# Opening the first SwiGLU with P1 and P2 of four groups, a second level one pair earlier, and P7 moved ahead of P2 in the values

## Chip, cores and metric

The kernel runs on one core of one Trainium2 chip. Its time is device microseconds (us) of one launch; of several runs the median is given. The engines are named as in the profile: PE (TensorE, matmuls), PEld (its weight loads), DVE (VectorE), ACT (ScalarE), POOL (GpSimd) and SP (SyncE, which here issues the loads and stores).

## What is computed

One layer of a streaming encoder on 1024 tokens of width 1024, in float32:

```python
h = x + 0.5 * swiglu(rmsnorm(x, g1), w1_in, w1_out)      # first SwiGLU, d_ff = 2816
u = rmsnorm(h, g_mix)
q, k, v, g_ret, p, gates = split(u @ w_in)               # "values" below is v
...                                                      # retention, pooling, merge
h = h + merged @ w_out
h = h + 0.5 * swiglu(rmsnorm(h, g2), w2_in, w2_out)
out = rmsnorm(h, g_final)
# swiglu(x) = (silu(x @ w_in[:, :2816]) * (x @ w_in[:, 2816:])) @ w_out
```

## The kernel before

**One matmul in float32.** A product of 128 weight columns by 512 tokens over 128 channels is made from three matmuls (`mm3`, lines 176 to 180): weights and operand are each split into a rounded high part (a cast on ScalarE, line 158) and a remainder (a subtraction on VectorE, line 159; lines 162 and 163 do the same with a scale), and high x high, high x low and low x high are added in PSUM.

**Groups.** The input half of a SwiGLU (`ffn_in`, line 693) has 22 groups of 256 output rows: 128 gate rows and 128 up rows, by 1024 tokens, over 1024 channels. With channels, rows and tokens each halved, a group is a 2 x 2 block product, made by Strassen's scheme in Winograd's form (`strassen`, line 425) with seven products, P1 to P7, instead of eight. Weight operands are L11, L12, L22 and the combinations S1 to S4; token operands are R11, R21, R22 and the combinations T1 to T4, made once and kept in 28 buffers (`mv`). One product is 12 matmuls of 512 columns. P1 and P2 (L11 x R11, L12 x R21) need only tokens as they come; P6 needs T2, P7 T3, P5 T1, P4 T4, P3 R22. P1 stands in a bank `a`, is copied to a bank `b` where P6, P5 and P3 are added, and P2 is added to it in `a`.

**Second level.** Two neighbouring groups together have one product (P3 over R22, or P2 over R21) that is again a 2 x 2 block product, and `common` (line 531) makes it with seven half products of 256 columns, 42 matmuls, instead of two products of 24 matmuls of 512. It needs the blocks of R22 or of R21 and their differences (`blocks`), made once for all pairs and kept in buffers of the rings `tl` (4) and `t4` (9).

**Order in the first SwiGLU.** The first group is a plain one (`plain_group`, line 776): eight products of 12 matmuls, with no combinations, whose operands are R11, R21, R12, R22. Then `pairs_of_both` (line 610) takes the other 21: two groups side by side in the order P1, P2, P6, P7, P5, P4, P3 (`BY_OPERAND`), a third one alone, and nine pairs, of which the first three have a second level on P3 alone and the last six on both.

**Order of the work.** `Flow.run` takes the steps one by one: a step has a part that prepares its weights (done four steps ahead) and a body with its matmuls. Side work on the operands, norms and outputs waits in one queue, `flow`; after each body one piece of it is taken (two in some stages), and a body that needs an operand takes pieces until that operand is made. The order of instructions on each engine is fixed when the kernel is built, by this order as a priority, with later work moved up where an engine would wait; on the chip each engine keeps its order.

**Beginning.** Lines 1046 to 1069 load the plain group's weights and the halves of x (16 loads of 256 KB) from SP's queue and put the operands' work into `flow`, then eight `x_square` pieces (line 1069 on), which square x by tokens, and the norm's statistics: roots and a row of 1024 factors (`n1rb`), spread over the partitions with four matmuls. Before the row is there, a gate is copied out as it is and scaled at the group's end; then follow silu, the product with the up rows, and for each two groups the combinations that the output half needs (lines 746 to 758), stored to memory.

**Values.** The projection v (line 1222 on) is one block product of its own, its seven products in four steps each. P1, P6, P7 and P4 go into four banks `a`; P5, P3 and P2 into four banks `b`. The order was P1, P6 with P5, P3, P2, P7, P4. When P2 is done, the norm's statistics and the blocks of its R22 go into `flow`.

Of the kernel before, what the change touches and what calls it, by code (L numbers as in the profile page):

```python
# [90 lines left out]
def block_kernel(ctx: ExitStack, tc, x, x_tok, vecs, f1_in, f1_out, w_in, w_v, pool_w, w_ret, w_pool, w_o,  # L91
# [330 lines left out]
    class Group(list):  # L422
        pass

    def strassen(nx, wa, wb, name, evac, end, begin=None, shared=(), dest=None):

        t = {}

        def blocks():
            ra, rb = raw(f"{name}ra"), raw(f"{name}rb")
            load(ra, wa)
            load(rb, wb)
            t.update(L11=half(ra, 0), L12=half(ra, 1), L21=half(rb, 0), L22=half(rb, 1))
# [24 lines left out]

        def prod(dst, w, m, start, stop):
            for i in range(4):
                mm3(t[dst], parts(t["w", w], i), parts(nx.operand(m, i)), start and i == 0, stop and i == 3)

        def u(n):
            t[n] = c2(f"{name}{n}")
            return t[n]

        def b1():
            if begin:  # L470
                begin()
            t["a"] = bank(f"{name}a")
            prod("a", "L11", "R11", True, False)
            t["b"] = sum_bank(f"{name}b")
            with soon():
                copy(t["b"], t["a"])

        def b6():
            prod("b", "S2", "T2", False, False)
            with soon():  # L480
                copy(u("v"), t["b"])

        def fourth():

            if "b5" in t and "p7" in t:
                with soon():
                    evac((1, 1), t["b"], t["p7"])

        def b5():
            prod("b", "S1", "T1", False, False)  # L490
            t["b5"] = True
            fourth()

        def b7():
            t["e"] = bank(f"{name}e")
            prod("e", "S3", "T3", True, False)
            with soon():
                copy(u("p7"), t["e"])
            fourth()

        def b2():
            prod("a", "L12", "R21", False, True)
            with soon():
                evac((0, 0), t["a"], None)

        def b3():
            prod("b", "S4", "R22", False, True)
            with soon():
                evac((0, 1), t["b"], None)

        def b4():
            prod("e", "L22", "T4", False, True)
            with soon():
                evac((1, 0), t["e"], t["v"])

        def last(f):
            def go():
                f()
                t["ends"] = t.get("ends", 0) + 1
# [87 lines left out]

        return step[0], body

    def pairs_of_both(nx, groups, first, some):  # L610

        groups = list(groups)
        A, B = (g(()) for g in groups[:2])
        steps = [g[m] for m in first for g in (A, B)]
        n = 2
        if len(groups) % 2:
            C = groups[n](())
            steps += [C[m] for m in BY_SUM]
            n += 1
        tl_, t4_ = ("tl", N_TL), ("t4", N_T4)  # L620

        steps[-1] = then(steps[-1], nx.blocks("R22", [t4_, tl_, t4_], True))
        yield from steps
        for k, n in enumerate(range(n, len(groups), 2)):
            A, B = (g((2, 3) if k >= some else (3,)) for g in groups[n : n + 2])
            yield A[0]
            yield B[0]
            if k < some:
                yield A[4]
                yield then(B[4], nx.blocks("R21", [tl_] * 3, True)) if k == some - 1 else B[4]  # L630
            elif k > some:
                yield from common(nx, A, B, 2)

            yield from (A[3], A[1], B[3], B[1], A[2], B[2])
            if k != some:
                yield from common(nx, A, B, 3)
                yield A[6]
                yield B[6]
            else:
                yield from common(nx, A, B, 2)  # L640
                yield A[6]
                yield B[6]
                yield from common(nx, A, B, 3)
# [46 lines left out]
            yield prep, body  # L690


    def ffn_in(nx, w, ops, name, start=None):

        R, T, B, T4 = ops
        hid = {}
# [1 line left out]
        def group(g):  # L698
            gate_up = {}

            def dest(which):
                tile, j = which
                if tile not in gate_up:
                    gate_up[tile] = (tl if start and g == 0 else t4)(f"{name}{'gu'[tile]}{g}")
                return half(gate_up[tile], j)

            later = []
# [53 lines left out]

                flow.add(w1, w1b, w2, w3)

            if start and g == 0:
                return plain_group(nx, start, f"{name}{g}_", evac, end)
            return lambda shared: strassen(nx, w[g, 0], w[g, 1], f"{name}{g}_", evac, end, shared=shared, dest=dest)

        done = ops_done.setdefault(name, set())
        order = [g for k in range(FH) for g in (k, k + FH)]
        if start:  # L770
# [5 lines left out]
    def plain_group(nx, blocks, name, evac, end):  # L776

        t, w = {}, {}

        def step(o, i, j):  # L780


            def prep():
                if j == 0:
                    w[o, i] = weights(blocks[2 * o + i], f"{name}w{o}{i}")

            def body():
                if i == 0:
                    t[o] = bank(f"{name}{o}{j}")
                for k in range(4):  # L790
                    mm3(t[o], parts(w[o, i], k), parts(nx.operand(("R11", "R12", "R21", "R22")[2 * i + j], k)),
                        i == 0 and k == 0, i == 1 and k == 3)
                if i == 1:
                    evac((o, j), t[o], None)
                    if (o, j) == (1, 1):
                        end()

            return prep, body

        return [step(o, i, j) for j in range(2) for i in range(2) for o in range(2)]  # L800

    ops_done = {}

# [252 lines left out]
    load(lead[0], f1_in[0, 0, :, :H])  # L1056
# [164 lines left out]
    def values():  # L1221
# [690 lines left out]
```

## Time and profile before

| | us |
|---|---|
| median of 3 runs | 2156.06 |
| lowest and highest of them | 2154.53, 2156.15 |
| profiled execution | 2153.9 |
| span of its profile (first to last instruction) | 2152.1 |
| TensorE busy in the span | 2138.3 |
| VectorE busy | 1848.9 |
| ScalarE busy | 1092.7 |

The profile is of one execution. A row of the timeline gives start, duration, engine, line, operation, output <- inputs, and how many were merged (x), with the idle time before and what ended it in brackets. A row of the waits gives who waited for whom, the total, the number and the longest. A row of the windows gives a stretch, its length, and each engine's busy time in it with the number of instructions, then the granted TensorE clock, the DMA engines' busy share and GB/s. Names are those of the program without numbers: `a_` is the first SwiGLU's input half (`a_wS` a weight of a combination, `a_b`, `a_a`, `a_e`, `a_x`, `a_y` banks), `n1` its norm and operands (`n1R`, `n1T`), `vL` and `vS` the values' weights and banks.

### The profile page before, as it was taken

What the parts mean: (1) busy time and instruction counts of PE and PEld (TensorE: products, weight loads), DVE (VectorE), ACT (ScalarE), POOL (GpSimd) and SP (SyncE); (2) the same over time, 40 slices, a digit from 0 to 9 for tenths busy, and PEclk for the clock granted to TensorE, in tenths of its full rate; (3) what the DMA queues carried; (4) which work ended last, traced back from release to release, by engine and by line L of the source; (5) the groups of instructions that cost most, each with busy time, mean ns of one, the idle gap of its engine ahead of it and who ended that gap; (6) DMA issues with size and microseconds to landing.
All of it is one profiled execution on the core that took longest, in us unless ns stands there. A gap on an engine that the chain in (4) does not pass through costs nothing.

```text
span 2152.1 us, 29764 instructions
## 1 busy us (share of the span) xinstructions
PE 2138.3 (99%) x10686; PEld 1812.0 (84%) x10686; DVE 1848.9 (86%) x3248; ACT 1092.7 (51%) x2059; POOL 0.2 (0%) x4
## 2 busy tenths in 40 slices
PE   9999999999999999999999999999999999999998
PEld 7888888888887888888888898887888888888887
DVE  8798888997988689888888877899988888899796
ACT  8544444454654444444446754446644544445454
POOL 0000000000000000000000000000000000000000
PEclk9999999999999999999999999999999999999999
DMA  7232423585537233332336567634123232358542
GB/s 259 73 133 74 138 83 128 181 283 186 182 119 242 89 127 138 108 128 91 115 119 238 168 220 256 218 99 157 69 89 132 74 130 91 128 180 291 200 132 98
DMA packets 120131, 320.91 MB, mean 149 GB/s; under 512 B 13232, under 2 KB 17456, under 8 KB 119984
## 3 DMA queue, kind: packets, MB, share of 16 engines
q1 hardware_dynamic: 119408, 317.98, 43.0%
q8 instruction: 83, 1.36, 0.3%
q10 hardware_dynamic: 576, 1.05, 0.1%
q14 instruction: 64, 0.52, 0.1%
HBM read 228.27 MB, written 90.70 MB: 148 GB/s over the span
## 4 chain that ended last, share of the span: by engine, by line
PE 93%; DVE 3%; DMA 1%; ACT 1%; issue 1%; SPq 0%; DVEq 0%; ACTq 0%
PE c_b L178 2%; PE c_b L180 2%; PE c_b L179 2%; PE a_b L178 2%; PE a_b L179 2%; PE a_b L180 2%; PE c_e L178 2%; PE c_e L179 2%; PE c_e L180 2%; PE a_e L179 2%; PE a_e L178 2%; PE a_e L180 2%; PE c_a L179 1%; PE c_a L180 1%; PE c_a L178 1%; PE a_a L178 1%
## 5 line engine op out<-in xcount | busy, mean ns | idle before, releaser
L179 PE MATMUL c_b<-n3T,c_wS 128*128 128x512 f32 x176 | 68.5, 389 | 0.0
L180 PE MATMUL c_b<-n3T,c_wS 128*128 128x512 f32 x176 | 68.5, 389 | 0.0
L178 PE MATMUL c_b<-n3T,c_wS 128*128 128x512 f32 x176 | 68.1, 389 | 0.0
L178 PE MATMUL a_b<-n1T,a_wS 128*128 128x512 f32 x168 | 65.4, 389 | 0.0
L179 PE MATMUL a_b<-n1T,a_wS 128*128 128x512 f32 x168 | 65.4, 389 | 0.0
L180 PE MATMUL a_b<-n1T,a_wS 128*128 128x512 f32 x168 | 65.3, 389 | 0.0
L178 PE MATMUL a_a<-n1R,a_wL 128*128 128x512 f32 x120 | 46.7, 389 | 0.0
L179 PE MATMUL a_a<-n1R,a_wL 128*128 128x512 f32 x120 | 46.7, 389 | 0.0
L180 PE MATMUL a_a<-n1R,a_wL 128*128 128x512 f32 x120 | 46.7, 389 | 0.0
L179 PE MATMUL c_a<-n3R,c_wL 128*128 128x512 f32 x112 | 43.7, 390 | 0.0
L180 PE MATMUL c_a<-n3R,c_wL 128*128 128x512 f32 x112 | 43.6, 389 | 0.0
L178 PE MATMUL c_a<-n3R,c_wL 128*128 128x512 f32 x112 | 43.6, 389 | 0.0
L178 PEld LDWEIGHTS c_b<-n3T,c_wS 128*128 128x128 f32 x176 | 33.1, 188 | 6.9
L179 PEld LDWEIGHTS c_b<-n3T,c_wS 128*128 128x128 f32 x176 | 33.0, 188 | 6.9
L180 PEld LDWEIGHTS c_b<-n3T,c_wS 128*128 128x128 f32 x176 | 33.0, 188 | 6.8
L159 DVE TENSOR_TENSOR a_wS<-a_S,a_wS 128x512 fp32r<-128x512 f32 x45 | 30.8, 684 | 8.0 <-ACT a_wS L158 8.0
L180 PEld LDWEIGHTS a_b<-n1T,a_wS 128*128 128x128 f32 x168 | 31.5, 188 | 6.6
L178 PEld LDWEIGHTS a_b<-n1T,a_wS 128*128 128x128 f32 x168 | 31.5, 188 | 6.6
L179 PEld LDWEIGHTS a_b<-n1T,a_wS 128*128 128x128 f32 x168 | 31.5, 188 | 6.5
L159 DVE TENSOR_TENSOR c_wS<-c_S,c_wS 128x512 fp32r<-128x512 f32 x46 | 31.4, 682 | 3.7 <-ACT c_wS L158 3.6
L179 PE MATMUL c_e<-n3T,c_wL 128*128 128x512 f32 x88 | 34.4, 391 | 0.0
L178 PE MATMUL c_e<-n3T,c_wL 128*128 128x512 f32 x88 | 34.4, 391 | 0.0
(3109 smaller groups left out, 8059.6 us busy)
## 6 DMA issues: line engine op xcount, KB each, us to landing
c_ra<-in_f_in SPq DMA_DIRECT2D x22, 512.0 KB, 3.6
c_rb<-in_f_in SPq DMA_DIRECT2D x22, 512.0 KB, 4.3
a_ra<-in_f_in SPq DMA_DIRECT2D x21, 512.0 KB, 3.7
a_rb<-in_f_in SPq DMA_DIRECT2D x21, 512.0 KB, 4.5
t<-au SPq DMA_DIRECT2D x11, 512.0 KB, 4.1
b<-ag SPq DMA_DIRECT2D x11, 512.0 KB, 3.3
r<-au SPq DMA_DIRECT2D x11, 512.0 KB, 3.5
br<-r SPq DMA_DIRECT2D x11, 512.0 KB, 5.6
```

The lines of the kernel that those rows point to most:

```text
L159: tt(lo, src, hi.bitcast(F32), SUB)
L178: mm(dst, w[0], m[0], start=start, stop=False, skip_group_check=True)
L179: mm(dst, w[0], m[1], start=False, stop=False, skip_group_check=True)
L180: mm(dst, w[1], m[0], start=False, stop=stop, skip_group_check=True)
```

## The change

The first SwiGLU no longer has a plain group. Four groups (0, 11, 1, 12) make P1 and P2 first (`leading`): P1 goes from its bank to the half of the gate tile that P3 fills later, and is copied into bank `b` when P6 begins. Then the first two groups make their other products side by side, and the second two the rest of theirs as a pair with a second level on P3. The other nine pairs have second levels on both P2 and P3. The four gates stand in the ring `tl`, and `x_square` loads into `t4` instead. R12 isn't made any more. The loads at the beginning are ordered anew, and the work on R22 comes ahead of T2 in `flow`, with R22's own split last. The second SwiGLU is as it was. In the values, P7 comes before P2.

```diff
@@ strassen @@
-    def strassen(nx, wa, wb, name, evac, end, begin=None, shared=(), dest=None):
+    def strassen(nx, wa, wb, name, evac, end, begin=None, shared=(), dest=None, lead=None):
...
-                if n == "L11":
+                if "L11" not in t:
                     blocks()
-                elif n in ("S2", "S3") and "S1" not in t:
+                if n in ("S2", "S3") and "S1" not in t:
                     combine("S1", "L21", "L22", ADD)
...
+        def first(n):
+            def prep():
+                t["w", n] = weights(half(lead, n == "L12"), f"{name}w{n}")
+
+            def body():
+                if n == "L11":
+                    t["a"] = bank(f"{name}a")
+                    prod("a", n, "R11", True, False)
+                    with soon():
+                        copy(dest((0, 1)), t["a"])
+                else:
+                    b2()
+
+            return prep, body
+
         def b6():
+            if lead is not None:
+                t["b"] = sum_bank(f"{name}b")
+                with soon():
+                    copy(t["b"], dest((0, 1)))
             prod("b", "S2", "T2", False, False)
...
+        if lead is not None:
+            g[0], g[4] = first("L11"), first("L12")
@@ pairs_of_both @@
+    def leading(nx, groups):
+
+        A, B, C, D = (g(s) for g, s in zip(groups, ((), (), (3,), (3,))))
+        for m in (0, 4):
+            yield from (g[m] for g in (A, B, C, D))
+        rest = [g[m] for m in BY_OPERAND if m not in (0, 4) for g in (A, B)]
+        rest[-1] = then(rest[-1], nx.blocks("R22", [T4_, TL_, T4_], True))
+        yield from rest
+        yield from (C[3], C[1], D[3], D[1], C[2], D[2])
+        yield from common(nx, C, D, 3)
+        yield C[6]
+        yield then(D[6], nx.blocks("R21", [TL_] * 3, True))
...
-    def pairs_of_both(nx, groups, first, some):
+    def pairs_of_both(nx, groups, lead):
+
+        groups, some, n = list(groups), 0 if lead else 2, 4 if lead else 2
+        if lead:
+            yield from leading(nx, groups[:n])
+        else:
+            A, B = (g(()) for g in groups[:n])
...
@@ ffn_in @@
-                    gate_up[tile] = (tl if start and g == 0 else t4)(f"{name}{'gu'[tile]}{g}")
+                    gate_up[tile] = (tl if g in start and not tile else t4)(f"{name}{'gu'[tile]}{g}")
...
-            return chain(group(0), pairs_of_both(nx, (group(g) for g in order[1:]), BY_OPERAND, 3))
-        return pairs_of_both(nx, (group(g) for g in order), BY_OPERAND, 2)
+        return pairs_of_both(nx, (group(g) for g in order), start)
@@ beginning @@
-    ra, rb = raw("ra"), raw("rb")
-    lead = half(ra, 0), half(ra, 1), half(rb, 0), half(rb, 1)
+    lead = {g: raw(f"lead{g}") for g in (0, FH, 1, FH + 1)}
...
+    def leads(j, gs):
+        for g in gs:
+            load(half(lead[g], j), f1_in[g, 0, :, j * H : (j + 1) * H])
+
+    leads(0, (0,))
     quarters(0, range(4))
-    load(lead[2], f1_in[0, 1, :, :H])
-    load(lead[1], f1_in[0, 0, :, H:])
+    leads(0, (FH, 1, FH + 1))
     quarters(0, range(4, 8))
-    load(lead[3], f1_in[0, 1, :, H:])
+    leads(1, (0, FH))
+    quarters(1, range(4, 8))
+    leads(1, (1, FH + 1))
     quarters(1, range(4))
-    quarters(1, range(4, 8))
...
-    first.work(first.r11, first.r21, first.r12, first.r22, first.p22, first.t2, first.t3, first.t1, first.t4_)
+    first.work(first.r11, first.r21, first.r22, first.t2, first.t3, first.t1, first.t4_, first.p22)
...
-        r = tl(f"xs{t}")
+        r = t4(f"xs{t}")
@@ values @@
+        yield from product("S3", "T3", "a", False, result(1, 1, lambda i: old("f", i)))
         yield from product("L12", "R21", "b", True, result(0, 0, lambda i: p1s.pop(i)))
-        yield from product("S3", "T3", "a", False, result(1, 1, lambda i: old("f", i)))
         yield from product("L22", "T4", "a", False, result(1, 0))
```

More of the change, by code (lines that the diff above doesn't have):

```diff
@@ L608, in then @@
         return step[0], body
-    def pairs_of_both(nx, groups, first, some):
[L612 to L623, printed above, removed]
+    def leading(nx, groups):
[9 more added lines that the diff above has]
+        yield then(D[6], nx.blocks("R21", [TL_] * 3, True))
+    TL_, T4_ = ("tl", N_TL), ("t4", N_T4)
+    def pairs_of_both(nx, groups, lead):
[4 more added lines that the diff above has]
+            A, B = (g(()) for g in groups[:n])
+            steps = [g[m] for m in BY_OPERAND for g in (A, B)]
+            steps[-1] = then(steps[-1], nx.blocks("R22", [T4_, TL_, T4_], True))
+            yield from steps
         for k, n in enumerate(range(n, len(groups), 2)):
@@ L629, in pairs_of_both @@
                 yield A[4]
-                yield then(B[4], nx.blocks("R21", [tl_] * 3, True)) if k == some - 1 else B[4]
+                yield then(B[4], nx.blocks("R21", [TL_] * 3, True)) if k == some - 1 else B[4]
             elif k > some:
@@ L690, in plain, with ffn_in @@
             yield prep, body
-    def ffn_in(nx, w, ops, name, start=None):
+    def ffn_in(nx, w, ops, name, start={}):
         R, T, B, T4 = ops
@@ L762, in end @@
                 flow.add(w1, w1b, w2, w3)
-            if start and g == 0:
-                return plain_group(nx, start, f"{name}{g}_", evac, end)
-            return lambda shared: strassen(nx, w[g, 0], w[g, 1], f"{name}{g}_", evac, end, shared=shared, dest=dest)
+            return lambda shared: strassen(nx, w[g, 0], w[g, 1], f"{name}{g}_", evac, end, shared=shared, dest=dest,
+                                           lead=start.get(g))
         done = ops_done.setdefault(name, set())
         order = [g for k in range(FH) for g in (k, k + FH)]
-        if start:
-            return chain(group(0), pairs_of_both(nx, (group(g) for g in order[1:]), BY_OPERAND, 3))
-        return pairs_of_both(nx, (group(g) for g in order), BY_OPERAND, 2)
[L776 to L800, printed above, removed]
+        return pairs_of_both(nx, (group(g) for g in order), start)
     ops_done = {}
@@ L1054, in quarters @@
             load(first.tiles[mt, j], x[mt, :, j * H : (j + 1) * H])
-    load(lead[0], f1_in[0, 0, :, :H])
+    def leads(j, gs):
+        for g in gs:
+            load(half(lead[g], j), f1_in[g, 0, :, j * H : (j + 1) * H])
+    leads(0, (0,))
     quarters(0, range(4))
-    load(lead[2], f1_in[0, 1, :, :H])
-    load(lead[1], f1_in[0, 0, :, H:])
+    leads(0, (FH, 1, FH + 1))
     quarters(0, range(4, 8))
-    load(lead[3], f1_in[0, 1, :, H:])
+    leads(1, (0, FH))
+    quarters(1, range(4, 8))
+    leads(1, (1, FH + 1))
     quarters(1, range(4))
-    quarters(1, range(4, 8))
     load(cst, consts)
     flow.add(lambda: copy(ones_r, ones))
-    first.work(first.r11, first.r21, first.r12, first.r22, first.p22, first.t2, first.t3, first.t1, first.t4_)
+    first.work(first.r11, first.r21, first.r22, first.t2, first.t3, first.t1, first.t4_, first.p22)
     x_sums = eights("x_sums")
     def x_square(t):
-        r = tl(f"xs{t}")
+        r = t4(f"xs{t}")
         load(r, x_tok[t])
```

## Prediction

> **What bounds the kernel now.** I read the page first, then the matmuls in order of time, then the first SwiGLU cut into stretches.
>
> ```profile
> PE 2138.3 (99%) x10686; PEld 1812.0 (84%) x10686; DVE 1848.9 (86%) x3248; ACT 1092.7 (51%) x2059; POOL 0.2 (0%) x4
> ...
> PE 93%; DVE 3%; DMA 1%; ACT 1%; issue 1%; SPq 0%; DVEq 0%; ACTq 0%
> ```
>
> TensorE is busy 2138.3 of 2152.1 us and is 93% of the chain that ended last. So a change pays by the matmuls that it takes out and costs by the idle time that it puts in. The page's mean of 389 ns is no price for a matmul, since matmuls overlap; the price is the distance between starts:
>
> ```profile
> 149.81 0.39 PE L178 MATMUL a_b<-n1T,a_wS 128*128 128x512 f32 x1
> ...
> 152.53 0.28 PE L178 MATMUL a_x<-n1R,a_wx 128*128 128x256 f32 x1
> ...
> 157.38 0.39 PE L178 MATMUL a_e<-n1T,a_wL 128*128 128x512 f32 x1
> ```
>
> From 149.81 to 152.53 stand 12 matmuls of 512 columns (one product of a group): 0.2267 us each, 2.72 a product. From 152.53 to 157.38 stand the 42 half-width matmuls of one second level for a pair: 4.85 us, 0.1155 each.
>
> ```profile
> core 0: us, PE busy (x) PEld busy (x) DVE busy (x) ACT busy (x) POOL busy (x), PEclk, DMA share, GB/s
> 6.46:87.08 80.62, 80.33 (x352) 66.07 (x353) 65.94 (x115) 59.21 (x112) 0.00 (x0) 1.00 0.49 174
> 87.08:162.85 75.77, 75.74 (x374) 63.63 (x372) 70.14 (x125) 38.69 (x68) 0.00 (x0) 1.00 0.37 129
> 162.85:200.29 37.44, 37.44 (x187) 31.82 (x186) 31.00 (x58) 15.46 (x30) 0.00 (x0) 1.00 0.31 106
> 200.29:237.33 37.04, 37.04 (x205) 32.26 (x204) 33.96 (x67) 19.50 (x36) 0.00 (x0) 1.00 0.32 108
> 237.33:423.40 186.07, 185.69 (x1022) 161.25 (x1021) 160.31 (x283) 89.32 (x166) 0.00 (x0) 1.00 0.37 126
> ```
>
> These five stretches are the input half of the first SwiGLU: the plain group with three single groups; two pairs with one second level; a third such pair (37.44); the first pair with both levels (37.04); five more of those (37.21 each). TensorE has no slack in any of them, so matmuls taken out here shorten the end.
>
> **The change, part by part.** *Matmuls.* Before: 96 for the plain group, 3 x 84 for three groups, 3 pairs of 144 + 42 half-width, 6 pairs of 120 + 84 half-width: 1500 full and 630 half. After: 2 x 84, one pair of 144 + 42, 9 pairs of 120 + 84: 1392 full and 798 half. That is 108 x 0.2267 = 24.5 us out, and 4 x 4.85 = 19.4 us in: 5.1 us gained.
>
> The stretches give nearly the same. The four leading groups become 312 x 0.2267 + 4.85 + 0.9 (four matmuls that spread the norm) = 76.5; a first pair like 37.04 and eight at 37.21 make 334.7; with the 0.8 us of waits at the first matmuls (below) it is 412.0 against 416.94 now. I take **-4.9**.
>
> The Trainium skill ("TensorE: Matmul & The Clock Gate", Back-to-back issue gap) speaks against this: sustained with weight loads it gives 81 ns for 128 columns and 131 for 512, so by estimate 98 for 256. By it the edit costs 168 x 0.098 - 108 x 0.131 = +2.3 us. The rows above, 0.2267 and 0.1155, disagree, and the sum goes by them.
>
> *The values.* P7 moves ahead of P2.
>
> ```profile
> 677.33 0.39 PE L180 MATMUL vS<-vS4w,n2R 128*128 128x512 f32 x1
> 679.50 0.47 PE L178 MATMUL vL<-vL12w,n2R 128*128 128x512 f32 x1 [1.79 <-ACT vS3w L158]
> ```
>
> ```profile
> 678.07 0.69 DVE L1244 TENSOR_TENSOR vS<-vS 128x512 f32<-128x512 f32 x1 [0.52 <-DMA vS<-in_w_v]
> 678.68 2.47 DVE L1298 TENSOR_TENSOR vc<-vS,vh 128x512 f32<-128x512 f32 x4
> ```
>
> ```profile
> 669.98 2.47 SPq L137 DMA_DIRECT2D vL<-in_w_v  x4
> 672.97 3.44 SPq L137 DMA_DIRECT2D vS<-in_w_v  x6
> ```
>
> P2 (L12, R21) starts in the banks that P3 (S4, R22) has just ended. Its first matmul waits 2.17 - 0.23 = 1.9 us, until the first eviction at L1298 is through (678.68 + 0.69); the row's releaser, a cast of S3, isn't an input of it. VectorE was late because a combination for P7, with its load, stood ahead. With P7 between, which goes into the other banks, P2 has four products of 2.72 us more before it needs these: **-1.9**. P7's weights are then due 10.9 us earlier. Its loads take the place of vL at 669.98; the load issued at 672.97 ended VectorE's wait at 678.07, so 5 us from issue, and the first S3 lands near 675, plus combination, cast and remainder (0.6 each) 677, when P3 ends. Bounds 0 and 1.9; I take 0. The norm's statistics start one product (10.9 us) later; the next products work without them, and I cost that at nothing.
>
> *The opening queue on VectorE.*
>
> ```profile
> 6.46:29.05 22.59, 22.30 (x96) 18.02 (x97) 21.62 (x34) 19.62 (x34) 0.00 (x0) 1.00 0.88 340
> ```
>
> ```profile
> 4.59 0.69 DVE L159 TENSOR_TENSOR a_w<-ra,a_w 128x512 fp32r<-128x512 f32 x1 [1.89 <-ACT a_w L158]
> 37.31 1.89 DVE L159 TENSOR_TENSOR n1T<-x,n1T 128x512 fp32r<-128x512 f32 x3
> 45.38 2.08 DVE L163 SCALAR_TENSOR_TENSOR n1T<-n1t,vec,n1T 128x512 fp32r<-128x512 f32 x3
> ```
>
> ```profile
> 5.00:20.00 15.00, 13.78 (x60) 10.56 (x59) 13.23 (x21) 12.55 (x20) 0.00 (x0) 1.00 1.04 388
> 20.00:58.00 38.00, 38.00 (x169) 31.49 (x168) 35.81 (x59) 34.03 (x64) 0.00 (x0) 1.00 0.57 201
> ```
>
> The first row is the plain group: 22.59 us for 96 matmuls that take 21.76, so 0.8 of waits at the start. The first five loads stay as they are, so TensorE starts at 6.46 again, and its eight products end at 29.05 as now. The weights of P1 and P2 of four groups are eight loads of 256 KB instead of four, and the four groups load their blocks again (512 KB each, eight loads instead of six) once these buffers are free; both stand in SP's queue behind or between the quarters of x. But the T operands come sooner: T2 at the ninth product (29.05) instead of the thirteenth (39.93), everything after it 10.9 us earlier. VectorE is full already: 13.23 of 15 and 35.81 of 38 us. An operation takes 0.605 (1.89 = 2 x 0.605 + 0.68), a scaled one 0.665. Up to the last T3 operand it must do: 8 weights, R11 and R21 8, T2 12, T3 8, S1 to S3 of two groups 6, their S2 and S3 weights 4, and 3 weights that stand ahead in program order: 49, 16 of them scaled: 30.6 us. It starts at 4.59. Its idle time is 1.8 us as now, and 2.8 more because the last quarter of x ends as the 24th load instead of the 20th (four of 262 KB at 388 GB/s are 2.7 us): T3 ends at 39.8. TensorE then has two products' last quarters (1.4) left: 41.2 against 39.9 at its own pace: **+1.3** late. To the end of P3 of both groups come T1 4, T4 8, R22 4, S4 with weights 4, one L22 weight and two evictions: 72, 24 of them scaled, 45.0 us, and up to four operations (2.4) of the next groups. With 4.59, 4.6 of idle time and TensorE's last quarter (0.7) that is 54.9 to 57.3 against 29.05 + 10 x 2.72 = 56.3, so nothing is added there. Lower bound 0, if only what is due goes first. Upper bound 5.6: strictly in program order the last T4 is the 70th operation, ready at 53.0, where TensorE asks for it at 29.05 + 6.75 x 2.72 = 47.4. I take 1.4, near the lower, since the trace shows the matmuls' order (fixed at build time) filled with other products where an operand is late:
>
> ```profile
> 117.25 0.40 PE L179 MATMUL a_e<-n1T,a_wL 128*128 128x512 f32 x1
> 117.48 0.32 PE L178 MATMUL a_x<-n1R22y,a_ws 128*128 128x256 f32 x1
> 117.64 0.40 PE L180 MATMUL a_e<-n1T,a_wL 128*128 128x512 f32 x1
> ```
>
> Here P4 of a pair runs between the matmuls of its second level.
>
> *The gates in tl.* Four gate tiles now hold all four tl buffers, and one block of the second level (y2 of R22) needs one. The first free one is that of group 0, after the norm's row is there.
>
> ```profile
> 86.63 0.62 PE L246 MATMUL n11b<-n11dg,ones_r 128*128 128x512 f32 x2
> ```
>
> ```profile
> 87.31 0.59 ACT L406 COPY n1rb<-n11b 128x512 f32<-128x512 f32 x1
> 88.44 1.28 ACT L735 ACT_TABLE_LOAD   x1
> 89.73 1.06 ACT L735 ACTIVATE ag<-ag 128x1024 f32<-128x1024 f32 x1
> ```
>
> ```profile
> 87.94 1.23 DVE L727 TENSOR_TENSOR ag<-ag,n1rb 128x1024 f32<-128x1024 f32 x1 [1.90 <-ACT n1rb L406]
> 91.95 1.29 DVE L733 TENSOR_TENSOR au<-ag,au 128x512 f32<-128x512 f32 x2
> ```
>
> By program order the row's matmuls stand inside step one of that second level. From there: copy 0.59, scale 1.23, table 1.28, silu 1.06, products 1.29, two differences with remainders about 1.4: 6.9 us; with group 11's own chain on VectorE ahead (1.23 + 1.29 + 4 x 0.6) 11.8. TensorE has 12 half-width matmuls (1.4) before y2: 5.5 to 10.4 us to cover. P4 of the pair (5.4) and the first products of the next (5.4) can cover it, as at 117.25. Bounds 0 and 10.4; I take **+0.4**. If the cover goes, what is late next is all that follows in that pair.
>
> Each leading group's P1 goes out to the gate tile and back into a bank later, four copies more on ScalarE, which has 59.21 of 80.62 us busy here (first stretch above); they and x_square in t4 instead of tl are covered by TensorE's first products: nothing, unless the row comes late (its second half is due at about 77 us, before at 86.6).
>
> **Sum.** -4.9 - 1.9 + 1.4 + 0.4 = -5.0. The profiled execution took 2153.9 us (span 2152.1 and 1.8 around it), so that one would give 2148.9. It lies 2.2 below the median of the three runs, 2156.06; from the median: **2151.1**.
>
> About 0.2% (4.3 us, below 2151.75 or above 2160.4) is what a measurement of this kernel can tell from no change.
>
> **Rivals.** One row of the page is needed for the last of them.
>
> ```profile
> L178 PEld LDWEIGHTS a_b<-n1T,a_wS 128*128 128x128 f32 x168 | 31.5, 188 | 6.6
> ```
>
> 1. *VectorE's opening queue eats the gain*: waits of 3.5 to 5.6 us instead of 1.4 between 30 and 57 us. For it: VectorE full in both stretches. Against: TensorE filled its waits before. With 4.5 it is -1.9: 2154.2, within 0.2%.
> 2. *The values' wait moves* to P7's own weights, as their loads land just when due: +1.9 back: -3.1, 2153.0, within 0.2%.
> 3. *Slower: the gate tile.* y2 waits for group 0's gate with nothing to cover it: 10.4 us in place of 0.4: +5.0, 2161. It decides from 9.7 us of wait on. For it: the chain of 11.8 us; against: 10.9 us of other products. The Trainium skill ("TensorE: Matmul & The Clock Gate", What's actually happening) says that an idle window of about 3.4 us halves TensorE's clock until about 3.4 us of work; by estimate that would add 1.7 here. The rows of before have no such wait.
> 4. *Slower: half-width matmuls bound by their weight loads.* One weight load takes 0.188 us; at that distance 168 cost 31.9 for 24.5 taken out: +7.4 in place of -4.9, 2163. Against it: 15 second levels already run at 4.85. That price is also the nearest thing in rows to the Trainium skill's figure above (same page, Back-to-back issue gap).
>
> **How the numbers follow.** Forecast 0.46 (its own range 2149.2 to 2151.7, waits of 0 to 2.4 us together); rival 1 0.34; rival 2 0.09; rival 3 0.09; rival 4 0.02. So faster 0.46, same 0.43, slower 0.11. The range goes from 2148.5 (all waits at their lower bounds, and a little spread) to 2157.0, past rivals 1 and 2; above lie rivals 3 and 4, below almost nothing.
>
> **What would show it.** Matmuls: the first SwiGLU's input half ends near 418.5 instead of 423.4, with 168 more half-width matmuls. VectorE: TensorE's waits between 29 and 57 us on n1T or n1R add up to 1.4; 3.5 or more is rival 1. Gates: around 76 to 90 us, waits on n1R22y under 1 us; several us there with the gate's silu just before is rival 3. Values: no wait at the start of vL12w, and none at vS3w; a wait there is rival 2. Wrong altogether would be a 0.2267 or 0.1155 that changes, or waits far from these places.

## The result, and the profile after

| | before | after |
|---|---|---|
| median, us | 2155.45 (4 runs, 2154.53 to 2156.15) | 2183.49 (4 runs, 2181.25 to 2184.06) |
| profiled execution, its span | 2153.9, 2152.1 | 2181.25, 2179.5 |

The ratio is 1.0123, with a 95% interval of 1.0110 to 1.0135: the change makes the kernel **28 us slower**. The prediction said 2151.1, with a range to 2157.0.

The page of the kernel after, its engines and its chain:

```profile
PE 2145.5 (98%) x10746; PEld 1814.5 (83%) x10746; DVE 1868.9 (86%) x3287; ACT 1103.0 (51%) x2082; POOL 0.2 (0%) x4
...
PE 90%; DVE 7%; ACT 2%; issue 1%; DMA 1%; SPq 0%; DVEq 0%; ACTq 0%
```

There are 60 matmuls more, which is 168 half-width ones in and 108 full ones out, as counted. But TensorE's share of the chain falls from 93% to 90% and VectorE's rises from 3% to 7%. The first 153 us of both kernels, in the same stretches (length, busy time of PE, PEld, DVE, ACT, POOL, granted clock, DMA share, GB/s); before:

```profile
6.07:62.00 55.93, 55.25 (x242) 45.31 (x243) 51.99 (x88) 47.87 (x88) 0.00 (x0) 1.00 0.65 234
62.00:92.30 30.30, 30.30 (x136) 25.08 (x135) 18.33 (x33) 16.92 (x33) 0.00 (x0) 1.00 0.11 35
92.30:113.00 20.70, 20.70 (x93) 17.15 (x92) 20.63 (x36) 9.58 (x16) 0.00 (x0) 1.00 0.55 210
113.00:153.50 40.50, 40.47 (x202) 33.76 (x201) 37.38 (x73) 19.01 (x37) 0.00 (x0) 1.00 0.32 108
```

and after:

```profile
6.07:62.00 55.93, 48.69 (x190) 36.34 (x191) 45.32 (x71) 35.35 (x63) 0.00 (x0) 0.91 0.56 197
62.00:92.30 30.30, 30.24 (x142) 24.80 (x140) 18.92 (x38) 21.86 (x43) 0.00 (x0) 1.00 0.52 170
92.30:113.00 20.70, 7.72 (x24) 5.73 (x24) 17.87 (x39) 10.20 (x23) 0.00 (x0) 0.60 0.22 90
113.00:153.50 40.50, 37.96 (x199) 31.71 (x197) 39.70 (x80) 20.74 (x42) 0.00 (x0) 1.00 0.29 98
```

Read the first column after the length: TensorE is idle for 7.2, 13.0 and 2.5 us where it was never idle for more than 0.7. It waited for these (who, for whom, total, times, longest):

```profile
PE a_y L178 <- ACT n1R L158: 10.2, 1, 10.2
PE a_b L178 <- ACT n1T L158: 6.2, 1, 6.2
PE n11b L246 <- ACT n11dg L245: 1.8, 1, 1.8
PE a_b L178 <- ACT a_ws L158: 1.6, 1, 1.6
```

Idle time alone misses a part, since a matmul is busy for 0.39 us at a pitch of 0.2267. So I take the distance between the starts of neighbouring matmuls, less 0.2267 (512 columns) or 0.1133 (256), and add it up by stretch; below this is called the **loss**. Before: 0.8 us up to 62 us, 0, 0, and 1.0 from 113 to 160. After: 13.1, 0.4, 16.9 and 5.4. That is 34.0 us more, against 5.1 (matmuls) and 1.9 (values) gained: 27.0, and the spans differ by 27.4. Beyond 160 us the sums are 36.6 before, with the values' wait in it, and 36.0 after, so the two kernels agree there to about 1 us. So three places are to be explained: the T operands (to 62 us), the gap at 92 to 113, and R21's sums (113 to 160).

**The T operands.** VectorE around T2, after:

```profile
20.53 1.29 DVE L159 TENSOR_TENSOR a_wL<-lead,a_wL 128x512 fp32r<-128x512 f32 x2 [2.76 <-ACT a_wL L158]
23.35 0.69 DVE L439 TENSOR_TENSOR a_S<-a_rb 128x512 f32<-128x512 f32 x1 [1.52 <-DMA a_rb<-in_f_in]
...
27.68 0.69 DVE L159 TENSOR_TENSOR a_wS<-a_S,a_wS 128x512 fp32r<-128x512 f32 x1 [2.31 <-ACT a_wS L158]
...
30.94 0.69 DVE L318 TENSOR_TENSOR n1t<-x 128x512 f32<-128x512 f32 x1
```

The last row is the first operation that T2 needs. VectorE comes to it at 30.94, although it was idle for 2.76, 1.52 and 2.31 us in the 13 us before. (In e2 below, with the same loads, this operation starts at 21.52, so its input had landed.) TensorE's first product with T2 then stands at:

```profile
35.40 1.22 PE L178 MATMUL a_b<-n1T,a_wS 128*128 128x512 f32 x2 [6.18 <-ACT n1T L158]
```

**The gap at 92 to 113.** TensorE, and below it VectorE:

```profile
93.38 0.73 PE L246 MATMUL n10b<-n10dg,ones_r 128*128 128x512 f32 x2 [0.92 <-ACT n10dg L245]
95.96 0.96 PE L246 MATMUL n11b<-n11dg,ones_r 128*128 128x512 f32 x2 [1.85 <-ACT n11dg L245]
107.13 0.58 PE L178 MATMUL a_y<-n1R,a_ws 128*128 128x256 f32 x1 [10.21 <-ACT n1R L158]
```

```profile
97.58 2.36 DVE L759 TENSOR_TENSOR ag<-ag,n1rb 128x1024 f32<-128x1024 f32 x2 [2.04 <-ACT n1rb L406]
99.95 2.49 DVE L765 TENSOR_TENSOR au<-ag,au 128x512 f32<-128x512 f32 x4
...
105.02 1.29 DVE L356 TENSOR_TENSOR n1x<-n1R 128x512 f32<-128x512 f32 x2
```

The sums of R22's blocks (L356) need nothing of the norm's row; but they stand behind the gates of the first groups (L759, L765 and what follows), which do: in `flow` the gates' pieces come first. The row is 9 us later than before (n11b 95.96 against 86.63), since the loads of `x_square` are. The first and last of these eight loads in SP's queue, before and after:

```profile
16.85 1.03 SPq L137 DMA_DIRECT2D xs<-in_x_tok  x2
...
49.06 0.33 SPq L137 DMA_DIRECT2D xs<-in_x_tok  x1
```

```profile
54.22 9.79 SPq L137 DMA_DIRECT2D xs<-in_x_tok  x6
...
74.92 0.86 SPq L137 DMA_DIRECT2D xs<-in_x_tok  x2
```

The first goes out 37 us later and the last 26. The row is only 9 us later, because before it had time to spare: its last load was out at 49.06, and its matmuls stood at 83 to 87 us.

**The values.** No row of after has a wait at P2 (vL12w) or P7 (vS3w) any more, and none stands at P7's weights.

### The profile page after: what moved, and what is told of

It reads as the page before. It is cut to its first block, busy times and chain, and to the rows that moved or that the text cites. A ratio compares the mean times of both kernels' runs of the same rounds, so it can differ in the third digit from the quotient of the medians.

```text
span 2179.5 us, 29984 instructions
## 1 busy us (share of the span) xinstructions
PE 2145.5 (98%) x10746; PEld 1814.5 (83%) x10746; DVE 1868.9 (86%) x3287; ACT 1103.0 (51%) x2082; POOL 0.2 (0%) x4
## 4 chain that ended last, share of the span: by engine, by line
PE 90%; DVE 7%; ACT 2%; issue 1%; DMA 1%; SPq 0%; DVEq 0%; ACTq 0%
PE c_b L178 2%; PE c_b L180 2%; PE c_b L179 2%; PE a_b L178 2%; PE a_b L179 2%; PE a_b L180 2%; PE c_e L179 2%; PE c_e L178 2%; PE c_e L180 2%; PE a_e L178 1%; PE a_e L179 1%; PE a_e L180 1%; PE bp6b L180 1%; PE bp6b L178 1%; PE bp6b L179 1%; PE c_a L179 1%
## 5 line engine op out<-in xcount | busy, mean ns | idle before, releaser
L178 PE MATMUL a_b<-n1T,a_wS 128*128 128x512 f32 x176 | 69.7, 398 | 6.2 <-ACT n1T L158 6.2
L179 PE MATMUL a_b<-n1T,a_wS 128*128 128x512 f32 x176 | 69.7, 396 | 0.0
L180 PE MATMUL a_b<-n1T,a_wS 128*128 128x512 f32 x176 | 69.4, 395 | 0.0
L178 PEld LDWEIGHTS a_b<-n1T,a_wS 128*128 128x128 f32 x176 | 33.5, 191 | 14.6 <-ACT n1T L158 7.0
L178 PE MATMUL a_a<-n1R,a_wL 128*128 128x512 f32 x104 | 41.5, 399 | 0.8 <-ACT n1R L162 0.7
L179 PE MATMUL a_a<-n1R,a_wL 128*128 128x512 f32 x104 | 41.4, 398 | 0.3 <-DVE n1R L163 0.3
L180 PE MATMUL a_a<-n1R,a_wL 128*128 128x512 f32 x104 | 41.0, 394 | 0.0
L179 PEld LDWEIGHTS a_b<-n1T,a_wS 128*128 128x128 f32 x176 | 33.7, 191 | 7.9 <-DVE n1T L159 0.9
L180 PEld LDWEIGHTS a_b<-n1T,a_wS 128*128 128x128 f32 x176 | 33.7, 192 | 7.0 <-DVE a_wS L159 0.2
L178 PE MATMUL a_e<-n1T,a_wL 128*128 128x512 f32 x88 | 34.0, 392 | 0.6 <-ACT n1T L158 0.6
L179 PE MATMUL a_e<-n1T,a_wS 128*128 128x512 f32 x88 | 34.5, 392 | 0.0
```

The lines of the kernel that those rows point to most:

```text
L178: mm(dst, w[0], m[0], start=start, stop=False, skip_group_check=True)
L179: mm(dst, w[0], m[1], start=False, stop=False, skip_group_check=True)
L180: mm(dst, w[1], m[0], start=False, stop=stop, skip_group_check=True)
```

## The experiments

They ran on three chips, each beside the kernel before, which took 2156.9 to 2157.4 us there (medians of 13 to 19 runs). The changed kernel wasn't run beside them; by the ratio above it is at 2183.7. Differences given with a range are worked out from the ratios, and the medians can differ from them by about 1 us. The expectations of the first eight runs give times as for a run of before of about 2155.5 to 2156, so the losses by stretch, from one profiled execution each, and the ratios count more than the last microsecond.

| kernel | median | ratio to before, 95% | loss to 62 | 62-92 | 92-113 | 113-160 |
|---|---|---|---|---|---|---|
| before | 2157.2 | 1 | 0.8 | 0.0 | 0.0 | 1.0 |
| after | (2183.7) | 1.0123 (1.0110 to 1.0135) | 13.1 | 0.4 | 16.9 | 5.4 |
| e1_values | 2156.1 | 0.9996 (0.9987 to 1.0005) | 1.5 | 0.0 | 0.0 | 1.0 |
| e2_early_t | 2169.3 | 1.0060 (1.0043 to 1.0077) | 15.1 | 1.6 | 0.5 | 3.5 |
| e3_early_x | 2180.2 | 1.0106 (1.0091 to 1.0121) | 18.8 | 2.5 | 5.5 | 5.5 |
| e4_filled | 2184.9 | 1.0133 (1.0118 to 1.0148) | 6.3 + 5.9 | 2.0 | 15.8 | 6.2 |
| e6_second | 2159.4 | 1.0011 (1.0002 to 1.0020) | 1.3 | 0.0 | 0.0 | 3.8 |
| e7_rate2 | 2183.3 | 1.0125 (1.0112 to 1.0139) | 12.4 | 1.2 | 15.2 | 6.3 |
| e8_xs_t4 | 2160.3 | 1.0020 (1.0010 to 1.0030) | 1.3 | 3.3 | 0.0 | 0.8 |
| e9_best | 2174.3 | 1.0083 (1.0069 to 1.0097) | 13.0 | 1.5 | 5.3 | 5.5 |
| e10_no_low | 2173.7 | 1.0078 (1.0061 to 1.0095) | 5.3 | 13.7 | 2.5 | 5.2 |
| e11_loads | 2165.6 | 1.0038 (1.0023 to 1.0053) | 6.4 | 4.1 | 0.8 | 5.4 |
| e12_loads_later | 2158.4 | 1.0005 (0.9996 to 1.0015) | 6.3 | 4.1 | 0.4 | 0.2 |
| e13_tuned | 2161.2 | 1.0020 (1.0011 to 1.0030) | 6.6 | 4.3 | 3.3 | 0.1 |

(5.9 in e4 is the time of its 26 added matmuls. A wait counts in the stretch in which it begins; in e10 the gap that after has from 96 us on begins at 88, so it stands in the column of 62 to 92.)

**First theory: the order.** T2's operations, and those of the row, stand behind others that wait.

*e1_values*: the kernel before with the two lines of the values swapped.

```diff
+        yield from product("S3", "T3", "a", False, result(1, 1, lambda i: old("f", i)))
         yield from product("L12", "R21", "b", True, result(0, 0, lambda i: p1s.pop(i)))
-        yield from product("S3", "T3", "a", False, result(1, 1, lambda i: old("f", i)))
```

> The kernel before with P7 ahead of P2 in the values alone. Theory (the step works by itself as summed, 1.9 us from the wait on the values' vL12w): 2153.5 us. Rival (the wait only moves, to P7's weights or to vS3w): no change, 2155.4 us.

Measured: -0.9 us, from -2.8 to +1.1. Both -1.9 and 0 lie in that, but the trace of this run shows a part of the rival. P2's wait is gone, and P7's weights have one in its place:

```profile
680.79 0.50 PE L179 MATMUL vL<-vS3w,n2T 128*128 128x512 f32 x1 [0.91 <-DVE vS3w L159]
```

So about half of the wait moved. In after neither wait is there; why P7's weights come in time there, and that the swap is worth 1.9 us, no run shows.

*e2_early_t*: the changed kernel, with more pieces of the operands' work after each of the first eight products.

```diff
-            flow.rate = 1
+            flow.rate = 4 if n < 12 else 1
```

> The changed kernel with the T sums and the loads and squares of x built at four times the rate in the first eight products, so that T2's first sum stands in VectorE's order right behind the load of x and ahead of the S sums of the next groups. The same operations, another order. Theory (order: T2 and the row of the norm stand behind operations that wait for something else): the wait for T2 falls from 6.2 us to at most 1.5, the granted clock stays at 1.00 after it, the row of the norm is there by about 70 us and the gap at 92 to 107 us goes: 24 to 28 us less than the changed kernel, 2155 to 2160 us. Rival (the amount of VectorE's work, as in the first rival of the prediction): the wait for T2 stays at 4 us or more, and the time stays above 2170 us.

Measured: 14.4 us less than after, and only half of the theory came true. The loss at 92 to 113 us went (16.9 to 0.5). But TensorE still waited for T2, now for the other operand of the same product:

```profile
PE a_b L178 <- ACT a_wS L158: 7.0, 1, 7.0
PE a_e L178 <- ACT a_wS L158: 2.6, 1, 2.6
```

T2 and T3 were early, and the S sums and weights stood behind them.

*e3_early_x*: only the loads and squares of x come earlier in `flow`, ahead of T2.

```diff
-    first.work(first.r11, first.r21, first.r22, first.t2, first.t3, first.t1, first.t4_, first.p22)
+    first.work(first.r11, first.r21, first.r22)
...
+    first.work(first.t2, first.t3, first.t1, first.t4_, first.p22)
```

> The changed kernel with only the loads and squares of x for the norm's row built earlier; T2's place is as it was. Theory (two separate losses, each by order): the wait for T2 stays at about 6.2 us with the halved clock behind it, the loss at 92 to 113 us goes (10.6 + 2 + 1 of waiting and 3 of the halved clock), about 17 us less: 2166 us. Rival (the sums of R22 come late from VectorE's load and not from the row): 0 to 3 us less, 2180 to 2183 us.

Measured: 3.5 us less; by time this was close to the rival's 0 to 3. The loss at 92 to 113 did fall by 11.4, as the theory said, but the T operands lost 5.7 more and the stretch after them 2.1. Here what was taken from one place came up at the others, so this order has the largest loss to 62 us of all.

*e4_filled*: 26 matmuls of R11's high part with itself, into a bank that nobody reads, fill the gap ahead of T2.

> The changed kernel with 26 matmuls more, into a bank that nobody reads, in the gap ahead of T2's first product (work that the output doesn't need). Theory (the idle time halves the granted clock): T2's first product starts at about 35.4 us as before, but the granted clock of the next 5.8 us is 1.00 instead of 0.50, the pitch 0.227 instead of 0.427, and 3.0 us go: 2180.5 us. Rival (T2's operands pace these matmuls, not the clock): 0, 2183.5 us.

The granted clock is the number after POOL:

```profile
29.06:35.40 6.34, 6.34 (x28) 4.90 (x27) 6.30 (x11) 3.16 (x6) 0.00 (x0) 1.00 0.24 84
35.40:41.24 5.84, 4.52 (x16) 2.83 (x17) 5.84 (x11) 2.10 (x4) 0.00 (x0) 1.00 0.00 0
```

In after the same stretches are:

```profile
29.06:35.40 6.34, 0.16 (x2) 0.01 (x1) 6.30 (x12) 3.38 (x6) 0.00 (x0) 0.69 0.29 84
35.40:41.24 5.84, 5.84 (x13) 3.94 (x14) 5.84 (x10) 2.12 (x4) 0.00 (x0) 0.50 0.00 0
```

So the idle time does halve the clock, and filling it keeps it at 1.00; but no time was gained (2184.9). At 1.00 TensorE is idle in the second stretch and has run 16 matmuls instead of 13: VectorE is busy for all 5.84 us in both, which fits it setting the pace. The halved clock was a consequence here; no cost of its own shows.

*e7_rate2*: two pieces after each of the first eight products, so that T2's sums alternate with the S sums.

```diff
+            flow.rate = 2 if n < 12 else 1
```

> The changed kernel with two pieces of the operands' work instead of one after each of the first eight products: T2's sums now alternate with the S sums and their weights, neither stands behind all of the other. The row of the norm is left as late as in the changed kernel. Theory (order): the wait for T2 falls from 6.2 us to at most 2.5, and T1, T3, T4 add at most 2; the loss at 92 to 113 us for the row stays: 2176 to 2179 us. Rival (the amount of VectorE's work): the waits of 29 to 62 us stay at 8 us or more together, and the time at 2181 us or more.

Measured: 2183.3, the rival. The wait for T2 fell from 6.2 to 1.2 us, exactly as the order theory wanted, and the loss to 62 us stayed (12.4 for 13.1). **The order theory fell for this place**: this order takes the wait for T2 away and leaves the sum. Other orders of the same operations made the sum larger (15.1 in e2, 18.8 in e3), so an order can cost here; none with these loads took it below 12.4.

**Second theory: the amount, and when it can start.** VectorE's work up to the last T operand doesn't fit, because VectorE can do too little before. Its busy time up to T2, and TensorE's in the time after it, in the kernel before:

```profile
4.50:29.06 24.56, 23.34 (x102) 18.32 (x101) 22.33 (x35) 20.45 (x36) 0.00 (x0) 1.00 0.89 337
29.06:62.00 32.94, 32.94 (x147) 27.29 (x146) 30.35 (x55) 27.86 (x53) 0.00 (x0) 1.00 0.48 160
```

in e7_rate2:

```profile
4.50:29.06 24.56, 23.70 (x100) 18.03 (x99) 14.81 (x22) 17.39 (x31) 0.00 (x0) 1.00 0.94 338
29.06:62.00 32.94, 26.86 (x99) 18.18 (x98) 31.97 (x52) 19.58 (x35) 0.00 (x0) 0.95 0.33 110
```

VectorE has done 14.8 us of work by 29.06 instead of 22.3, and from then on it is full (31.97 of 32.94). In before R12 landed earlier, and T2's first difference began at 14.44:

```profile
14.44 0.69 DVE L318 TENSOR_TENSOR n1t<-x 128x512 f32<-128x512 f32 x1
```

In after most of VectorE's idle time from 4 to 31 us ended with a cast on ScalarE:

```profile
DVE a_wL L159 <- ACT a_wL L158: 6.5, 6, 2.8
```

Another 2.3 us ended with the first cast of `a_wS`, which stood on ScalarE behind a copy of P2 that had waited 1.94 us for TensorE. So ScalarE's order may have a share in the late start; no run separates it from the loads.

*e10_no_low*: e7 without the 16 subtractions on VectorE that make the remainders of T1 to T4, so its products are only nearly right.

```diff
+            if self.name == "n1" and n[0] == "T":
+                ...
+                self.high.add((n, i))
...
+                if (m, i) in nx.high:
+                    x = x[0], parts(nx.operand("R11", i))[1]
```

> The kernel with two pieces a step, where the remainders of T1 to T4 are left out (16 subtractions on VectorE, 0.60 to 0.66 us each, 10 us in all; the low part of R11 stands in for them, so the products are only nearly those of the reference). TensorE's matmuls, the casts and the loads stay. Theory (from 20 to 60 us VectorE has more work than TensorE's pace allows, in any order): TensorE's waits before 62 us fall from 12.4 to 2 to 4 us, 2174 us. Rival (the loads or ScalarE's queue pace the T operands): 0 to 2 us less, 2181 to 2183 us.

Measured: 2173.7, where the theory said 2174. The loss to 62 us fell from 12.4 to 5.3, a little less than the theory said (2 to 4), and TensorE's busy time there rose:

```profile
29.06:62.00 32.94, 30.88 (x131) 23.75 (x130) 30.19 (x49) 28.47 (x53) 0.00 (x0) 1.00 0.51 177
```

*e9_best*: e7 with two pieces a step for longer, and four `x_square` loads go into buffers that the last T operands need only later; no tile of x has to be free for them.

```diff
+    def x_early(t):
+        x_load(t, sb.tile([P, S], F32, tag="mv", bufs=N_MV, name=f"xs{t}"))
```

> The changed kernel with two pieces after each of the first products, and the first four x_square loads in buffers of the operands' ring that T4 and R22 use only later, issued ahead of the next groups' weights; the squares stand behind T4's sums, the other four loads behind the first four squares. Theory (both losses were order alone): no wait over 2 us for T2, the row there by 60 us, no gap at 92 to 107 us; what is left is up to 5 us of R21's sums near 135 to 150 us: 2155 to 2160 us by the run of before of that chip at 2156 or so. Rival (VectorE's work in the first 150 us is too much in any order): 2165 us or more.

Measured: 2174.3, the rival. Most of the row's part went (16.9 to 5.3 at 92 to 113 us), the T operands' loss stayed at 13.0.

*e11_loads*: e9, with R12 loaded ahead of R21 and R22, T1 (which needs R12 and R11 alone) made while R22 is on its way, and four pieces a step up to T2.

```diff
-    leads(0, (FH, 1, FH + 1))
+    leads(0, (FH, 1))
+    quarters(1, range(4))
+    leads(0, (FH + 1,))
     quarters(0, range(4, 8))
...
-    quarters(1, range(4))
...
+    first.work(first.r11, first.d1, first.r21, first.t1, first.r22, first.t2, first.t3)
```

> The kernel with the x_square loads in free buffers, and besides the other order of the beginning: R12's quarters load before R21's and R22's, R22's before the last two L12 weights; the differences of R12 and R11 and T1 are made before R22 is there, four pieces a step up to T2 and two after it. So VectorE has work in its first 20 us, where it was idle for 5.7 of 15.5 us. Theory (VectorE's work was late because it could start only late): the waits before 62 us fall from 13 to at most 4 us, 9 us less than that kernel: 2165 us. Rival (the amount alone, wherever it starts, or P2's operands late in exchange): 2171 us or more.

Measured: 2165.6, as the theory said (2165), though the loss to 62 us is 6.4 and not at most 4. The operations are the same, but VectorE can start on them. Below are e9, then e11:

```profile
4.50:29.06 24.56, 23.80 (x99) 18.08 (x98) 14.43 (x22) 17.36 (x31) 0.00 (x0) 1.00 1.01 369
```

```profile
4.50:29.06 24.56, 23.20 (x98) 17.43 (x97) 21.71 (x34) 21.47 (x38) 0.00 (x0) 1.00 0.94 330
29.06:62.00 32.94, 31.32 (x128) 24.63 (x127) 30.59 (x52) 27.21 (x51) 0.00 (x0) 0.95 0.55 198
```

That is 7.3 us more of VectorE's work before 29.06, and 6.6 us less loss before 62. Three things changed together; four pieces a step without the other two (e2) had a loss of 15.1.

**The row and the sums of R21.**

*e8_xs_t4*: the kernel before with one line of the change.

```diff
-        r = tl(f"xs{t}")
+        r = t4(f"xs{t}")
```

> The kernel before with one line of the change: the tiles of x_square come from the ring t4, which x itself fills, instead of tl. Theory (these loads wait for x's tiles to be free, and the row comes late): 6 to 15 us more than before, with TensorE's wait near 75 to 95 us on the row or on what follows from it. Rival (the row has slack enough there, and its lateness came from SP's queue behind the weights of the next groups): 0 to 2 us more.

Measured: +4.3 us (2.2 to 6.5), between the two. The cause is as the theory says: with no other change the first load goes from 16.85 to 51.13 and the last from 49.06 to 72.83,

```profile
51.13 11.29 SPq L137 DMA_DIRECT2D xs<-in_x_tok  x7
...
72.83 0.42 SPq L137 DMA_DIRECT2D xs<-in_x_tok  x1
```

and TensorE waits for the row (1.6 and 0.7 us), whose last matmuls start at 89.89 for 86.63. The size was too high: no common product follows right behind the row in that kernel, so the sums of R22 cost nothing there (a loss of 0.0 from 92 to 113 us).

*e6_second*: the kernel before with its second level on P2 two pairs earlier.

```diff
-            return chain(group(0), pairs_of_both(nx, (group(g) for g in order[1:]), BY_OPERAND, 3))
+            return chain(group(0), pairs_of_both(nx, (group(g) for g in order[1:]), BY_OPERAND, 1))
```

> The kernel before, with the plain group, where the second level on P2 begins two pairs earlier (one pair with a single second level instead of three). Two pairs then have 42 half-width matmuls in place of 24 full ones each. Theory (the matmuls' price as summed): 2 x (5.44 - 4.85) less, so 1.2 us, if R21's sums aren't late: 2154.5 us. Rival (R21's sums are late there as in the changed kernel): 3 to 5 us more.

Measured: +2.4 us (0.4 to 4.3), the rival's side. The 1.2 us of matmuls are more than paid back by 2.8 us of loss at 113 to 160, where VectorE has R21's sums to make beside the weights:

```profile
128.11 0.50 PE L180 MATMUL a_a<-n1R,a_wL 128*128 128x512 f32 x1 [1.51 <-DVE a_wL L159]
```

*e12_loads_later*: e11, with R21's sums and the second level on P2 one pair later.

```diff
-        yield then(D[6], nx.blocks("R21", [TL_] * 3, True))
+        yield D[6]
...
-        groups, some, n = list(groups), 0 if lead else 2, 4 if lead else 2
+        groups, some, n = list(groups), 1 if lead else 2, 4 if lead else 2
```

> The same, and the second level on P2 begins one pair later (24 full matmuls for 42 half ones: 0.6 us more), so that R21's sums come after R22's with one pair between. Theory (both sets of sums beside the weights of the pair fill VectorE from 92 to 150 us): the waits from 113 to 160 us, 5 us, go: 2 to 4 us less than without, 2161 to 2163 us. Rival (the sums only move to a place where VectorE is as full): no gain, or 1 us more.

Measured: 2158.4, 7.2 us less and more than expected; 5.2 of it is the loss at 113 to 160, which went. The rest lies behind 160 us in the two traces and within the spread of the two kernels' runs. This version has all parts of the change but one pair's second level on P2, with loads, T1 and `x_square` in another order, and is level with before: +1.1 us, from -0.9 to +3.2.

*e13_tuned*: e12 with four small waits taken away (x_square's loads later, one piece a step from the 16th step on, L12 ahead of two quarters of R21, P2's copies without priority).

> The last kernel with what still waited in it, 10.8 us before 95 us: the loads of x_square after T4's sums; one piece a step again from the 16th step on, so that the roots and the row of the norm aren't asked for in one step (0.7 and 1.2 us on n10dg and n11dg); L12's first weights before R21's last two quarters (0.6 and 0.4 us); and the copies of P2 out of its bank, which stood ahead of the cast of S2's weights on ScalarE, lose their priority (1.4 us on a_wS and about 2 us of the halved clock behind it). Theory: 3 to 6 us of these go, 2152 to 2155 us by a run of before of 2157, so 2 to 5 us faster than before. Rival (VectorE is full to 62 us, so a wait taken away comes back later): 0 to 2 us less, 2156.5 to 2158.5 us, the same as before.

Measured: 2161.2, 2.8 us more than e12 and worse than theory and rival. The waits on the row's parts went, others took their place:

```profile
PE a_b L178 <- ACT a_wS L158: 2.5, 4, 1.3
PE a_y L178 <- ACT n1R L158: 1.3, 2, 1.0
```

No kernel that ran is shown to beat before. Open stays whether another order of the first 60 us could (e12 has 6.3 us of loss there, for 0.8 in before), and what the swap in the values is worth in the changed kernel.

## Why the prediction was wrong, step by step

- **Matmuls, -4.9: right.** 60 more in the count, and the price held: a pair with both levels takes 37.14 us in after (191.88 to 229.02) for 37.04 and 37.21 before. So weight loads set no bound (rival 4, whose 168 x 0.188 is 31.6 and not 31.9).
- **The values, -1.9:** in after the wait is gone and rival 2's isn't there. Alone (e1) it measured -0.9, with 0 inside the interval, and 0.9 us of rival 2's wait is in the trace; the term for P7's weights, taken at 0, was 0.9 there.
- **The opening queue on VectorE, +1.4 with bounds 0 and 5.6: the step that failed first.** It cost 12.3 us (13.1 less 0.8). The operations were counted well; the idle time was not. "Its idle time is 1.8 us as now, and 2.8 more" stands there, 4.6 us; between 4.50 and 29.06 it was 10.0 (24.56 less the 14.52 us that VectorE is busy in after). And the 1.8 is the idle time from 5 to 20 us alone; from 20 to 58 us before has 2.2 more. Taking the plain group away also took away what VectorE did in these 23 us: R12's own split, R22's, T2's differences, which began at 14.44. The new order makes R12 the last of x's quarters, and nothing of T2 can begin without it. The upper bound used the same idle time, so it was none. Rival 1 had this mechanism, at a chance of 0.34, but with 3.5 to 5.6 us, by the same idle time. e10 (less work) and e11 (an earlier start) each took away about 7 of the 12 us; e7's order alone took none. What the other 5 us are stays open.
- **The cover for T2.** That other products fill the wait where an operand is late was taken from a later place (117.25). Here all four groups had made P1 and P2, and no product but P3, the last, does without a T operand.
- **x_square in t4, "nothing, unless the row comes late": it came late,** and this was the largest loss, 16.9 us. How much of it goes depends on how early the row is: with its last matmuls at 79 to 85 us 5.3 to 5.5 are left (e9, e3), at 66 to 68 us 0.5 to 0.8 (e2, e11). The text named the due time (77 us; it came at 95.96) but not the tiles of x that the loads must wait for, nor SP's queue.
- **The gates in tl, +0.4:** y2 did not wait for a gate for long. Rival 3, at a chance of 0.09, had the place and the size (10.4 us for 10.2, by chance) but not the mechanism: y1 waited, whose sums stand behind the gates on VectorE, and these waited for the row.
- **R21's sums one pair earlier: not in the sum at all.** They cost 4.4 us in after (5.4 less 1.0) and 2.8 in e6, and this loss is gone in e12.
- **The clock.** The granted clock was 0.50 from 35.40 to 41.24 after 6.2 us of waiting, and again after the 10.2. The Trainium skill ("TensorE: Matmul & The Clock Gate", What's actually happening) says that about 3.4 us of idleness halve it; the trace agrees on the half. Rival 3 charged 1.7 us for that; in e4 no such cost shows at T2, where the operands pace TensorE. For the second place that wasn't tried.
- VectorE kept its order in the rows shown for the T operands: T2's first operation, with its input landed, started behind remainders that waited for casts and that it doesn't need. The Trainium skill (the same page, the table at its head) calls the queues of VectorE and ScalarE strict FIFO, and the rows at 20.53 to 30.94 agree.

## What to carry to other kernels

Work that is taken off the engine that bounds the kernel may be what hid another engine's start-up: before cutting it, list what that other engine can do in each stretch with the data that has landed by then, and count its idle time anew, not from the old trace. When an experiment removes one wait and the sum of waits stays (e7), look for the engine that is full behind them all; here less work (e10) and an earlier start (e11) helped. And of a buffer that moves to another ring, ask what holds that ring's tiles, and what stands behind the load in its queue.

## What had not been expected of the hardware

The clock was also halved without any long idle time. In e12 TensorE is busy for 1.40 of 3.00 us, in pieces, with no wait over 1.2 us; then:

```profile
32.00:35.00 3.00, 1.40 (x6) 0.54 (x5) 3.00 (x6) 3.00 (x7) 0.00 (x0) 1.00 0.26 26
35.00:36.00 1.00, 1.00 (x4) 0.68 (x5) 1.00 (x3) 0.96 (x2) 0.00 (x0) 0.64 0.49 160
36.00:38.00 2.00, 2.00 (x6) 1.62 (x5) 2.00 (x4) 0.44 (x1) 0.00 (x0) 0.50 1.03 412
```

In four kernels (e7, e9, e11, e12) the 3.41 us ahead of such a drop hold only 1.63 to 1.83 us of busy TensorE, with no wait over 1.5 us. The Trainium skill ("TensorE: Matmul & The Clock Gate", What's actually happening) speaks of an idle window of about 3.4 us; here a stretch that is half idle was enough. No limit follows from these runs: waits of 1.3 us in e13 at the same place left the clock at 1.00.

Nor did full speed come back after a fixed time of work: 6.3 us after TensorE had begun again in after (35.40 to 41.67), 4.0 us in e2 (36.64 to 40.61). In the first 200 us of all these traces the time at half speed is a whole multiple of 3.41 us: once that at the four places above, twice in e2 (6.83), three and five times in after:

```profile
31.43:41.67 10.24, 6.27 (x14) 4.28 (x15) 10.24 (x18) 4.37 (x9) 0.00 (x0) 0.50 0.05 21
96.28:113.35 17.07, 6.87 (x22) 5.41 (x21) 14.99 (x29) 6.93 (x12) 0.00 (x0) 0.50 0.27 108
```
